# A two-layer hybrid block on one core: weights of products of 256 columns moved 64 bytes off the grid of 256, weight buffers in a strict ring, and VectorE alone updating x behind the output projection

## The chip, the core and the metric

The kernel runs on one core of a Trainium2 chip. The metric is the device time of one execution in microseconds, here the median of three runs. The core's engines work side by side, each through its own list of instructions in order: TensorE (PE in the profile; its weight loads have a line of their own, PEld), VectorE (DVE), ScalarE (ACT), GpSimd (POOL) and SyncE (SP), whose queue issues the weight transfers here.

## The reference

Two layers over 512 tokens of width 1024. Cut to what matters:

```python
h = rms_norm(x, g_pre_mix)
q, k, v, qi, ki, wi, xr, gr, zu, zv, gate_logits = split(h @ w_in)
y_a = dsa_attention(q, k, v, qi, ki, wi)        # indexer picks keys per query
y_b = rg_lru(conv(xr)) * gelu(gr)               # a linear recurrence over tokens
y_c = gelu(zu) * spatial(rms_norm(gelu(zv)))    # masked 128x128 products by chunk
merged = sum_n sigmoid(gate_n) * (y_n @ w_branch_n)
x = x + rms_norm(merged @ w_out, g_post_mix)
f = square(relu(rms_norm(x, g_pre_ffn) @ w_ffn_up)) @ w_ffn_down
x = x + rms_norm(f, g_post_ffn)
x = x + rms_norm((p @ w_ple) * sigmoid(x @ w_ple_gate), g_post_ple)
```

All of it is float32.

## The kernel before

**Layout.** x lies transposed in SBUF: eight tiles X0 to X7 of 128 features by 512 tokens. A product with 128 output columns is a sum over eight k-blocks. To keep float32's precision every operand is split in a high part (rounded to the format that TensorE takes) and the low rest, and each block is three matmuls (`mm3`, L360 to L363): xh·wh, xh·wl, xl·wh. The 128x128 weight block is the operand that is loaded into the array, and the tokens stream through, 512 columns (a wide product) or 256 (a narrow one, half of the tokens). In the spatial products of the gMLP branch it is the other way round: there the weights stream.

**Weights.** A list `order` gives every weight chunk (128x1024, 512 KB) in the order of its use. `prep` (L242) takes the next: a transfer on SP's queue into one of three raw buffers `wr`, a cast on ACT to the high part `wh` (L253) and a subtraction on DVE for the low part `wl` (L254). There are four buffers of each kind (NWB = 4), handed out as they come free, so `wh` and `wl` of one chunk need not lie side by side; chunks of the branches, which serve two products, keep theirs longer while others rotate. All of these tiles, and those that hold x's parts, start at multiples of 512 bytes. `getw(key, ahead)` hands out the weights of the next product and preps up to `ahead` (3) chunks beyond.

**Order of the work.** The program is written in PE's order, with a clock of its own (`clk`, moved on by `tick`) by which deferred pieces are put between the matmuls: `defer(us, fn)` runs `fn` that much later, `run_later` does it. Extra dependencies that cost no waiting (`weights_first`, `behind_products`) keep the scheduler from moving a weight split or a root ahead or back.

**The stage of the change.** Out 0 to 4 of the output projection are wide. Out 5 to 7 go by halves of the tokens (`gemm_halves`, L384): 3 x 24 narrow matmuls for the first 256 tokens, then as many for the others; each of the second three ends with a `prep`. Behind each, `out_evac` squares the sum for the norm's statistics and copies it to Y with the gain (ACT L455 and L1153). When a half is complete, `Norm.complete` gets its 1/rms (`rstd_tok`), brings it to all partitions by two transposes on PE (`rstd_bc`, L497), and starts the generator `x_tiles` (L537), which for tile d writes

```python
V.tensor_mul(ys[d][:, r], ys[d][:, r], bc)              # L544, DVE
(G if d in on_g else V).tensor_add(X[d][:, r], X[d][:, r], ys[d][:, r])  # L547
A.activation(hi, x, AF.Copy, scale=g[:, d:d + 1])       # L557, ACT: xh
st.square(x, r)                                         # L455, ACT
st.accumulate(r)                                        # L461, POOL: sum of squares
V.scalar_tensor_tensor(lo, x, g[:, d:d + 1], f32v(hi), op0=ALU.mult, op1=ALU.subtract)  # L567: xl
```

with the update of tile d + 1 between the square and the accumulation. With `on_g=(1, 3, 5)` POOL does the adds of these three tiles; the accumulations are all POOL's. `gemm_arriving` (L398) takes the tiles as they come for the first four chunks of the FFN's up projection (matmuls L419, 24 narrow ones per chunk and half): three chunks with every tile, the fourth from the second tile on, and the last three tiles of the second half chunk by chunk. The next norm's statistics (`Stats`, L440; `st2` here) are summed alongside. The same two functions serve the last three gate chunks of a layer and the first three chunks (xr 0 to 2) of layer 1.

**Elsewhere.** The recurrence of the RG-LRU branch (L942) runs on ACT and DVE beside the products of the gates and of attention: per feature tile tanh, exp, square, later four square roots in one block (L957). Sigmoid, exp, tanh and root need tables on ACT; a change of table is an ACT_TABLE_LOAD.

Of the kernel before, what the change touches and what calls it, by code (L numbers as in the profile page):

```python
# [9 lines left out]
F32R = mybir.dt.float32r  # L10
# [40 lines left out]
def hybrid_block_kernel(ctx, tc, xT, pT, pos, vec, bsp, freq, w_in, w_tok, w_lru, w_sp, w_br, w_out, w_up, w_dn, w_ple, w_gate, out, depth=DEPTH, dbg=None):  # L51
# [11 lines left out]
    def nm(p):  # L63
        uid[0] += 1
        return f"{p}_{uid[0]}"
# [168 lines left out]
            order.append((("gate", l, d), w_gate[l, d]))  # L234

    prepared = {}
    LA = NWB - 1
    nprep = [0]
    nget = [0]

    def prep():
        weights_first()  # L242
        i = nprep[0]
        nprep[0] += 1
        key, src = order[i]
        raw = wp.tile([128, 1024], F32, tag="wr", name=nm("wr"), bufs=3)
        nc.sync.dma_start(raw, src)
        if key[0] == "sp":
            r3 = raw.rearrange("p (g t) -> p g t", g=8)
            G.affine_select(out=r3, in_=r3, compare_op=ALU.is_ge, fill=0.0, base=0, pattern=[[0, 8], [1, 128]], channel_multiplier=-1)  # L250
        hi = wp.tile([128, 1024], F32R, tag="wh", name=nm("wh"), bufs=NWB)
        lo = wp.tile([128, 1024], F32R, tag="wl", name=nm("wl"), bufs=NWB)
        A.copy(hi, raw)  # L253
        V.tensor_sub(lo, raw, f32v(hi))  # L254
        prepared[key] = (hi, lo)
        if not strict[0]:
            return
        ins = nc.cur_bb.bb.instructions
        parts[:] = [len(ins)] + [next(i.name for i in reversed(ins) if i.engine == e) for e in ENG]
# [125 lines left out]
    def gemm_halves(keys, xs, evac, done):  # L385


        ws = [getw(key, LA if i == 0 else 0) for i, key in enumerate(keys)]
        for r in HALVES:
            for i, w in enumerate(ws):  # L390
                ps = bank()[:, :S // 2]
                gemm(ps, w, xs, KT, r=r)
                evac(i, r, ps)
                if r is HALVES[1] and nprep[0] < len(order):
                    prep()
            done(r)

    def gemm_arriving(keys, xs, source, ranges, arrived=None, lag=LAG, tail=TAIL):  # L398


        n = len(keys)
        ws = [getw(key, 0) for key in keys[:-1]]
        pss = [bank() for _ in keys]
        last = {}
        for r in ranges:
            gen = source(r)
            for k in range(KT):
                with ordered(last):
                    next(gen)
                    todo = [(o, k) for o in range(len(ws))]  # L410
                    if len(ws) < n and k == lag:
                        ws.append(getw(keys[-1], 0))
                        todo += [(n - 1, q) for q in range(k + 1)]
                    if r is ranges[-1] and k >= KT - tail:
                        todo = [] if k < KT - 1 else [(o, q) for o in range(n) for q in range(KT - tail, KT)]
                    for i, (o, q) in enumerate(todo):
                        h3, l3 = [v.rearrange("p (k c) -> p k c", k=KT) for v in ws[o]]
                        for m in range(3):
                            PE.matmul(pss[o][:, r], (h3, l3, h3)[m][:, q], xs[q][m // 2][:, r], start=q == 0 and m == 0, stop=q == KT - 1 and m == 2)  # L419
                        if r is ranges[-1] and q == KT - 1 and o < n - 1:  # L420
                            prep()
                tick(0.65 * len(todo) * width(r) / S)
            if arrived is not None:
                arrived(r)
        while nprep[0] < nget[0] + LA:
            prep()
        return pss
# [12 lines left out]
    class Stats:  # L440


        def __init__(self, late=()):


            self.late = late
            self.n = {}
            self.q = {}
            self.ps = {}
            self.rt = small(4, "rt", 4)  # L450
# [7 lines left out]
        def accumulate(self, r=FULL):  # L458
            n = self.n[r.start, r.stop]
            if 0 < n < (KT - 1 if r in self.late else KT):  # L460
                G.tensor_add(sacc[:, r], sacc[:, r], self.q[r.start, r.stop])  # L461
            self.n[r.start, r.stop] = n + 1

        def add(self, src, r=FULL):
# [109 lines left out]
    chunks = []  # L574
    for key, src in order[:3]:
        raw = wp.tile([128, 1024], F32, tag="wr", name=nm("wr"), bufs=3)
        hi = wp.tile([128, 1024], F32R, tag="wh", name=nm("wh"), bufs=NWB)
        lo = wp.tile([128, 1024], F32R, tag="wl", name=nm("wl"), bufs=NWB)
        prepared[key] = (hi, lo)
        chunks.append((src, raw, hi, lo))  # L580
    nprep[0] = 3
# [19 lines left out]
    for l in range(depth):  # L601
# [544 lines left out]
        yb = [slot("K0", F32, True), slot("K1", F32, True)]  # L1146
        Y = [yb[d // 4][:, d % 4] for d in range(8)]
        st = Stats()
        st2 = Stats()

        def out_evac(d, r, ps):
            st.add(ps, r)
# [2 lines left out]
        for d in range(5):  # L1155
            ps = bank()
            gemm(ps, getw(("out", l, d)), M, KT)
            out_evac(d, FULL, ps)
        norm = Norm(st, D, lambda r, bc: x_tiles(r, XS, vc[:, V_FFN:V_FFN + 8], st2, Y, bc, on_g=(1, 3, 5)))
        gemm_halves([("out", l, d) for d in (5, 6, 7)], M, lambda i, r, ps: out_evac(5 + i, r, ps), norm.complete)  # L1160


        R = cp.tile([128, S], F32, tag="R", name=nm("R"))
        first = gemm_arriving([("up", l, 0, i) for i in range(4)], XS, norm.source, HALVES, st2.row(D, R))
        ps = bank()
        gemm(ps, getw(("up", l, 0, 4)), XS, KT)
        first.append(ps)
        run_later(force=True)
        H = {}
# [168 lines left out]
```

## Time and profile before

| what | value |
|---|---|
| runs | 1815.8, 1817.12, 1817.33 us; median 1817.12 |
| the profiled execution | 1815.54 us |
| its span in the profile | 1813.8 us (1.74 us lie outside it) |
| granted TensorE clock, mean | 0.997 |
| PE busy | 1789.2 us, 99% |
| DVE, ACT, POOL busy | 1149.9 us (63%), 787.3 us (43%), 340.8 us (19%) |
| chain that ended last | PE 75%, DVE 14%, POOL 4%, ACT 4%, issue 3% |
| DMA | 167.75 MB, 92 GB/s in the mean |

How to read it: the span goes from the first to the last recorded instruction. A busy time is the union of the recorded durations; matmuls are pipelined and overlap, so two of them are compared by their starts. A row of the timeline has the start, the duration, engine, line and operation, out<-in by the program's names without buffer numbers, and in brackets the idle time of the engine before it and what ended it. A row of the windows has for each engine the busy time and the number of instructions in the stretch, then the granted clock (1.00 is full), the share of the DMA engines, and GB/s.

### The profile page before, as it was taken

What the parts mean: (1) busy time and instruction counts of PE and PEld (TensorE: products, weight loads), DVE (VectorE), ACT (ScalarE), POOL (GpSimd) and SP (SyncE); (2) the same over time, 40 slices, a digit from 0 to 9 for tenths busy, and PEclk for the clock granted to TensorE, in tenths of its full rate; (3) what the DMA queues carried; (4) which work ended last, traced back from release to release, by engine and by line L of the source; (5) the groups of instructions that cost most, each with busy time, mean ns of one, the idle gap of its engine ahead of it and who ended that gap; (6) DMA issues with size and microseconds to landing.
All of it is one profiled execution on the core that took longest, in us unless ns stands there. A gap on an engine that the chain in (4) does not pass through costs nothing.

```text
span 1813.8 us, 22748 instructions
## 1 busy us (share of the span) xinstructions
PE 1789.2 (99%) x8748; PEld 1497.5 (83%) x8748; DVE 1149.9 (63%) x1946; ACT 787.3 (43%) x1289; POOL 340.8 (19%) x277
## 2 busy tenths in 40 slices
PE   9999999999999999999999999999999999999997
PEld 7888788888988888888888888788889888888886
DVE  8789987656375254534688899876565743544345
ACT  6547246554443222223546473466534422222233
POOL 0612123200420000002454131332004100000033
PEclk9999999999999999999999999999999999999998
DMA  5312322222222232332222222322222323222321
GB/s 176 105 60 97 105 93 94 70 82 82 93 93 94 95 103 93 96 113 86 91 80 99 69 94 84 114 82 70 82 93 70 105 95 103 93 97 102 105 82 58
DMA packets 49676, 167.75 MB, mean 92 GB/s; under 512 B 6048, under 2 KB 8864, under 8 KB 49568
## 3 DMA queue, kind: packets, MB, share of 16 engines
q1 hardware_dynamic: 47376, 163.64, 27.3%
q10 hardware_dynamic: 2192, 2.67, 0.4%
q8 instruction: 68, 1.11, 0.3%
q14 instruction: 40, 0.33, 0.1%
HBM read 164.19 MB, written 2.10 MB: 92 GB/s over the span
## 4 chain that ended last, share of the span: by engine, by line
PE 75%; DVE 14%; POOL 4%; ACT 4%; issue 3%; DMA 0%; SPq 0%; POOLq 0%; ACTq 0%; DVEq 0%
PE ps L361 22%; PE ps L363 22%; PE ps L362 22%; PE ps L419 4%; DVE wl L254 3%; DVE tmp L794 2%; DVE m L792 2%; PE ps L668 2%; PE ps L1060 1%; POOL tmp L653 1%; ACT wh L253 1%; PE ps L1046 1%; POOL sacc L461 1%; PE ps L759 1%; POOL tmp L654 1%
## 5 line engine op out<-in xcount | busy, mean ns | idle before, releaser
L253 ACT CAST wh<-wr 128x1024 fp32r<-128x1024 f32 x303 | 317.2, 1050 | 476.9 <-PE ps L363 397.1
L254 DVE TENSOR_TENSOR wl<-wr,wh 128x1024 fp32r<-128x1024 f32 x303 | 379.2, 1254 | 199.7 <-ACT wh L253 199.3
L361 PE MATMUL ps<-xh,wh 128*128 128x512 f32 (+1 forms) x1296 | 502.5, 388 | 0.0
L363 PE MATMUL ps<-xl,wh 128*128 128x512 f32 (+1 forms) x1296 | 495.4, 382 | 0.0
L362 PE MATMUL ps<-xh,wl 128*128 128x512 f32 (+1 forms) x1296 | 495.2, 382 | 0.0
L363 PEld LDWEIGHTS ps<-xl,wh 128*128 128x128 f32 x1296 | 243.6, 188 | 47.7
L361 PEld LDWEIGHTS ps<-xh,wh 128*128 128x128 f32 x1296 | 243.8, 188 | 45.7 <-issue 1.9
L362 PEld LDWEIGHTS ps<-xh,wl 128*128 128x128 f32 x1296 | 244.1, 188 | 43.3
L461 POOL TENSOR_TENSOR sacc<-sacc,tmp 128x256 f32<-128x256 f32 (+1 forms) x92 | 98.0, 1065 | 884.6 <-issue 584.5
L363 PE MATMUL ps<-V,wh 128*128 128x512 f32 (+1 forms) x528 | 195.4, 370 | 0.0
L363 PE MATMUL ps<-B,wh 128*128 128x512 f32 x336 | 131.1, 390 | 0.0
L361 PE MATMUL ps<-A,wh 128*128 128x512 f32 x320 | 125.0, 390 | 0.0
L362 PE MATMUL ps<-A,wl 128*128 128x512 f32 x320 | 124.5, 389 | 0.0
L1197 DVE TENSOR_TENSOR M<-M,ps 128x512 f32<-128x512 f32 x48 | 33.0, 688 | 141.3 <-PE ps L363 141.3
L1185 DVE TENSOR_TENSOR tmp<-ps,R 128x512 f32<-128x512 f32 x64 | 43.8, 690 | 112.1 <-PE ps L363 109.5
L363 PEld LDWEIGHTS ps<-V,wh 128*128 128x128 f32 x528 | 99.5, 188 | 16.8
L361 PE MATMUL ps<-K,wh 128*128 128x512 f32 x256 | 99.6, 389 | 0.0
L362 PE MATMUL ps<-K,wl 128*128 128x512 f32 x256 | 99.6, 389 | 0.0
L419 PE MATMUL ps<-xl,wh 128*128 128x256 f32 (+1 forms) x264 | 86.2, 326 | 5.5 <-DVE xl L567 5.1
L419 PE MATMUL ps<-xh,wl 128*128 128x256 f32 (+1 forms) x264 | 84.1, 319 | 0.8 <-DVE wl L254 0.8
L419 PE MATMUL ps<-xh,wh 128*128 128x256 f32 (+1 forms) x264 | 84.5, 320 | 0.1
L363 PEld LDWEIGHTS ps<-B,wh 128*128 128x128 f32 x336 | 63.1, 188 | 13.4
(243 smaller groups left out, 2835.7 us busy)
## 6 DMA issues: line engine op xcount, KB each, us to landing
wr<-in_w_in_dram SPq DMA_DIRECT2D x95, 512.0 KB, 3.3
wr<-in_w_up_dram SPq DMA_DIRECT2D x64, 512.0 KB, 3.2
wr<-in_w_dn_dram SPq DMA_DIRECT2D x64, 512.0 KB, 3.2
wr<-in_w_br_dram SPq DMA_DIRECT2D x24, 512.0 KB, 3.2
wr<-in_w_tok_dram SPq DMA_DIRECT2D x16, 512.0 KB, 3.2
wr<-in_w_out_dram SPq DMA_DIRECT2D x16, 512.0 KB, 3.2
wr<-in_w_gate_dram SPq DMA_DIRECT2D x16, 512.0 KB, 3.2
X<-in_xT_dram SPq DMA_DIRECT2D x8, 256.0 KB, 5.7
```

The costliest lines, as they stand in the source:

```text
L253: A.copy(hi, raw)
L254: V.tensor_sub(lo, raw, f32v(hi))
L361: PE.matmul(ps, wh, xh, start=start, stop=False)
L362: PE.matmul(ps, wl, xh, start=False, stop=False)
L363: PE.matmul(ps, wh, xl, start=False, stop=stop)
L419: PE.matmul(pss[o][:, r], (h3, l3, h3)[m][:, q], xs[q][m // 2][:, r], start=q == 0 and m == 0, stop=q == KT - 1 and m == 2)
L461: G.tensor_add(sacc[:, r], sacc[:, r], self.q[r.start, r.stop])
L668: PE.matmul(ps, x, w, start=k == 0 and i == 0, stop=k == KT - 1 and i == 2)
L792: V.max(m8, (sc if r == 0 else wk)[:, :n])
L794: V.match_replace(wk[:, :n], m8, (sc if r == 0 else wk)[:, :n], -3.0e38)
L1185: V.tensor_mul(t, ps, R)
L1197: V.tensor_add(F[d], F[d], ps)
```

## The change

It does four things.

1. *Homes.* `home(key)` replaces the two kinds of buffers by one ring of four, used strictly in turn, high and low part side by side in one tile of 2064 or 2096 columns. Keys in the set `narrow` (spatial, out 5 to 7, gate 5 to 7, up 0 to 3, and in layer 1 xr 0 to 2) start 64 bytes off a multiple of 256 (before or behind it); all others start at a multiple of 256, which in two of the four buffers is 256 past a multiple of 512.
2. *Guests.* Up 1 to 3, the second to fourth weights of the arrival stage, lie in twelve slots that belong to A0 to A7 and B0 to B3, high and low part in two slots each. These slots start at multiples of 512 bytes. Their split is two casts and two subtractions of 128x512.
3. *Splits early.* At the start of the halves of out, `gemm_halves` defers the preps of those three by 0.3, 2.7 and 5.1 us; before, they stood in the second half, one behind each product. The fifth up chunk is fetched with one chunk less ahead.
4. *DVE alone.* `on_g` is dropped for the update behind the output projection, and `st2` sums on DVE.

The diff, cut to its core:

```diff
+    HOMES = [(("A0", "A1"), ("A2", "A3")), (("A4", "A5"), ("A6", "A7")), (("B0", "B1"), ("B2", "B3"))]
+    guests = {}
+    for l in range(depth):
+        guests.update({("up", l, 0, i + 1): HOMES[i] for i in range(3)})
...
+    narrow = set()
+    for l in range(depth):
+        narrow.add(("sp", l))
+        narrow.update(("out", l, d) for d in (5, 6, 7))
+        narrow.update(("gate", l, d) for d in (5, 6, 7))
+        narrow.update(("up", l, 0, i) for i in range(4))
+        if l:
+            narrow.update(("in", l, f"xr{j}") for j in range(3))
+    ring = [0]
+
+    def home(key):
+        i = ring[0] % NWB
+        ring[0] += 1
+        t = wp.tile([128, 2064 if i % 2 else 2096], F32R, tag=f"wp{i}", name=nm("wp"))
+        c = 16 if (key in narrow) == (i % 2 == 0) else 0
+        return t[:, c:c + 1024], t[:, c + 1024:c + 2048]
...
-        hi = wp.tile([128, 1024], F32R, tag="wh", name=nm("wh"), bufs=NWB)
-        lo = wp.tile([128, 1024], F32R, tag="wl", name=nm("wl"), bufs=NWB)
-        A.copy(hi, raw)
-        V.tensor_sub(lo, raw, f32v(hi))
+        if key in guests:
+            hi, lo = [[slot(n, F32R) for n in part] for part in guests[key]]
+            for h in range(2):
+                split(raw[:, h * 512:(h + 1) * 512], hi[h], lo[h])
+        else:
+            hi, lo = home(key)
+            split(raw, hi, lo)
...
         ws = [getw(key, LA if i == 0 else 0) for i, key in enumerate(keys)]
+        n = sum(order[i][0] in guests for i in range(nprep[0], min(nprep[0] + 3, len(order))))
+        for i in range(n):
+            defer(0.3 + 2.4 * i, prep)
         for r in HALVES:
             for i, w in enumerate(ws):
                 ps = bank()[:, :S // 2]
                 gemm(ps, w, xs, KT, r=r)
                 evac(i, r, ps)
-                if r is HALVES[1] and nprep[0] < len(order):
+                if r is HALVES[1] and i >= n and nprep[0] < len(order):
                     prep()
...
-                G.tensor_add(sacc[:, r], sacc[:, r], self.q[r.start, r.stop])
+                self.eng.tensor_add(sacc[:, r], sacc[:, r], self.q[r.start, r.stop])
...
-        st2 = Stats()
+        st2 = Stats(eng=V)
...
-        norm = Norm(st, D, lambda r, bc: x_tiles(r, XS, vc[:, V_FFN:V_FFN + 8], st2, Y, bc, on_g=(1, 3, 5)))
+        norm = Norm(st, D, lambda r, bc: x_tiles(r, XS, vc[:, V_FFN:V_FFN + 8], st2, Y, bc))
...
-        gemm(ps, getw(("up", l, 0, 4)), XS, KT)
+        gemm(ps, getw(("up", l, 0, 4), LA - 1), XS, KT)
```

The scheduler settles where each instruction comes to stand; in all DVE's list grows from 1794 to 1840 rows, ACT's from 1217 to 1231 (six table loads among them), and POOL's shrinks from 282 to 242. Three places. First DVE at the beginning of the update behind layer 0's output projection (K is Y, ps the broadcast of 1/rms, X_176 to X_178 the tiles of x, wl and wr the weights). Before:

```order
L254 TENSOR_TENSOR wl_4352<-wr_4349,wh_4351 128x1024
L490 TENSOR_SCALAR sm_4467<-ps_4464 128x2
L254 TENSOR_TENSOR wl_4480<-wr_4477,wh_4479 128x1024
L544 TENSOR_TENSOR K_872_4172<-K_872_4172,ps_4499 128x256
L547 TENSOR_TENSOR X_176<-X_176,K_872_4172 128x256
L544 TENSOR_TENSOR K_872_4172<-K_872_4172,ps_4499 128x256
L254 TENSOR_TENSOR wl_4518<-wr_4515,wh_4517 128x1024
L567 SCALAR_TENSOR_TENSOR xl_13_188<-X_176,vec_79,xh_12_187 128x256
L544 TENSOR_TENSOR K_872_4172<-K_872_4172,ps_4499 128x256
L547 TENSOR_TENSOR X_178<-X_178,K_872_4172 128x256
L567 SCALAR_TENSOR_TENSOR xl_15_190<-X_177,vec_79,xh_14_189 128x256
L544 TENSOR_TENSOR K_872_4172<-K_872_4172,ps_4499 128x256
```

and after:

```order
L470 TENSOR_TENSOR B_842_4353<-wr_4349,B_840_4351 128x512
L470 TENSOR_TENSOR B_843_4354<-wr_4349,B_841_4352 128x512
L528 TENSOR_SCALAR sm_4417<-ps_4414 128x2
L582 TENSOR_TENSOR K_798_4098<-K_798_4098,ps_4443 128x256
L585 TENSOR_TENSOR X_176<-X_176,K_798_4098 128x256
L582 TENSOR_TENSOR K_798_4098<-K_798_4098,ps_4443 128x256
L585 TENSOR_TENSOR X_177<-X_177,K_798_4098 128x256
L605 SCALAR_TENSOR_TENSOR xl_13_188<-X_176,vec_79,xh_12_187 128x256
L582 TENSOR_TENSOR K_798_4098<-K_798_4098,ps_4443 128x256
L585 TENSOR_TENSOR X_178<-X_178,K_798_4098 128x256
L499 TENSOR_TENSOR sacc<-sacc,tmp_4510 128x256
L605 SCALAR_TENSOR_TENSOR xl_15_190<-X_177,vec_79,xh_14_189 128x256
```

The splits of the up weights (wl_4352 and those behind it) have moved up, in front of the statistics (sm), and lie in slots A and B; tile 1's add is now DVE's, and the sum of squares (sacc) stands in front of each low part.

Second, ACT in the recurrence of layer 0, where weights are cast (wh before, wp after). Before:

```order
L946 ACTIVATE B_338_1619<-B_310_1514,sp_289_1420 128x512
L253 CAST wh_1651<-wr_1649 128x1024
L947 ACT_TABLE_LOAD
L947 ACTIVATE B_310_1514<-B_310_1514,nsp_290_1422 128x512
L949 ACTIVATE tmp_1622<-B_310_1514 128x512
L253 CAST wh_1657<-wr_1655 128x1024
```

and after:

```order
L983 ACTIVATE B_312_1593<-B_284_1488,sp_266_1397 128x512
L469 CAST wp_1619<-wr_1617 128x1024
L984 ACT_TABLE_LOAD
L984 ACTIVATE B_284_1488<-B_284_1488,nsp_267_1399 128x512
L986 ACTIVATE tmp_1596<-B_284_1488 128x512
L469 CAST wp_1694<-wr_1692 128x1024
L469 CAST wp_1629<-wr_1627 128x1024
```

Between the weights 1619 and 1629 (1651 and 1657 before) a cast for a product further on, 1694 (1723 before, ten rows further down), has come to stand.

Third, ACT some rows further on, with the square roots of the recurrence (L957 before, L994 after) and a gate's tanh (L919, L956). Before:

```order
L253 CAST wh_1723<-wr_1721 128x1024
L949 ACTIVATE tmp_1707<-B_332_1603 128x512
L957 ACT_TABLE_LOAD
L957 ACTIVATE B_338_1619<-B_338_1619 128x512
L957 ACTIVATE B_353_1664<-B_353_1664 128x512
L957 ACTIVATE B_355_1682<-B_355_1682 128x512
L957 ACTIVATE B_359_1704<-B_359_1704 128x512
L919 ACT_TABLE_LOAD
L919 ACTIVATE tmp_1770<-tmp_1770 128x512
```

and after:

```order
L994 ACTIVATE B_312_1593<-B_312_1593 128x512
L956 ACT_TABLE_LOAD
L956 ACTIVATE tmp_1668<-tmp_1668 128x512
L984 ACTIVATE B_306_1577<-B_306_1577,nsp_267_1399 128x512
L994 ACT_TABLE_LOAD
L994 ACTIVATE B_324_1635<-B_324_1635 128x512
L986 ACTIVATE tmp_1678<-B_306_1577 128x512
L994 ACTIVATE B_326_1653<-B_326_1653 128x512
L956 ACT_TABLE_LOAD
L956 ACTIVATE tmp_1740<-tmp_1740 128x512
L994 ACT_TABLE_LOAD
L994 ACTIVATE B_330_1675<-B_330_1675 128x512
```

The four roots stood behind one table load; now they stand apart, with loads between them for tanh and exp.

## Rows read from the trace of the kernel before

**Rows 1.** The page, busy time of the engines (share of the span, instructions).

```profile
PE 1789.2 (99%) x8748; PEld 1497.5 (83%) x8748; DVE 1149.9 (63%) x1946; ACT 787.3 (43%) x1289; POOL 340.8 (19%) x277
```

**Rows 2.** Windows of stages; columns: window, length, busy (count) of PE, PEld, DVE, ACT, POOL, PEclk, DMA.

```profile
471.00:489.00 18.00, 18.00 (x152) 17.99 (x151) 4.75 (x7) 8.82 (x18) 6.38 (x8) 1.00 0.22 79
489.00:515.00 26.00, 24.59 (x199) 23.88 (x198) 23.00 (x44) 15.95 (x36) 18.09 (x21) 1.00 0.12 41
900.00:925.00 25.00, 21.49 (x153) 18.84 (x152) 22.42 (x44) 14.41 (x37) 19.38 (x23) 1.00 0.18 58
160.00:180.00 20.00, 20.00 (x90) 16.57 (x89) 18.13 (x37) 18.60 (x26) 5.89 (x5) 1.00 0.29 102
200.00:225.00 25.00, 23.56 (x102) 18.54 (x101) 23.96 (x39) 6.65 (x10) 4.98 (x4) 1.00 0.32 106
```

**Rows 3.** Timeline of PE, wide products; columns: start, duration (us), engine, line, operation.

```profile
470.32 0.39 PE L361 MATMUL ps<-M,wh 128*128 128x512 f32 x1
...
471.00 0.28 PE L361 MATMUL ps<-M,wh 128*128 128x256 f32 x1
```

**Rows 4.** Timeline of PE, narrow products of the output projection.

```profile
478.08 0.28 PE L363 MATMUL ps<-V,wh 128*128 128x256 f32 x1
...
478.80 0.28 PE L363 MATMUL ps<-V,wh 128*128 128x256 f32 x1
```

**Rows 5.** Timeline of PE, weight loads with two columns streamed each, near the end.

```profile
1794.31 0.59 PE L471 MATMUL ps<-ones,tmp 128*128 128x2 f32 x4
1794.76 0.36 PE L361 MATMUL ps<-xh,wh 128*128 128x256 f32 x1
```

**Rows 6.** Timeline of PE, the broadcast in the halves of out, and the matmul behind them.

```profile
484.76 0.38 PE L497 MATMUL ps<-ident,rt 128*128 128x128 f32 x2
...
488.92 0.28 PE L419 MATMUL ps<-xh,wh 128*128 128x256 f32 x1
```

**Rows 7.** Timeline of DVE, update of x behind the output projection, layer 0.

```profile
486.02 0.42 DVE L544 TENSOR_TENSOR K<-K,ps 128x256 f32<-128x256 f32 x1
486.47 0.42 DVE L547 TENSOR_TENSOR X<-X,K 128x256 f32<-128x256 f32 x1
486.81 0.41 DVE L544 TENSOR_TENSOR K<-K,ps 128x256 f32<-128x256 f32 x1
...
489.21 0.47 DVE L567 SCALAR_TENSOR_TENSOR xl<-X,vec,xh 128x256 fp32r<-128x256 f32 x1
489.61 0.41 DVE L544 TENSOR_TENSOR K<-K,ps 128x256 f32<-128x256 f32 x1
...
490.58 0.47 DVE L567 SCALAR_TENSOR_TENSOR xl<-X,vec,xh 128x256 fp32r<-128x256 f32 x1
...
510.20 1.35 DVE L567 SCALAR_TENSOR_TENSOR xl<-X,vec,xh 128x256 fp32r<-128x256 f32 x2
```

**Rows 8.** Timeline of ACT, same stage: a cast of weights, the square of X1.

```profile
489.76 1.05 ACT L253 CAST wh<-wr 128x1024 fp32r<-128x1024 f32 x1
490.70 0.42 ACT L455 ACTIVATE tmp<-X 128x256 f32<-128x256 f32 x1
```

**Rows 9.** Timeline of DVE, the last update of x.

```profile
1805.68 1.27 DVE L546 SCALAR_TENSOR_TENSOR B<-B,gp,ps 128x256 f32<-128x256 f32 x3 [1.35 <-PE ps L497]
```

**Rows 10.** Timeline of ACT, recurrence of layer 0: a table load.

```profile
173.32 1.28 ACT L957 ACT_TABLE_LOAD   x1
```

**Rows 11.** Timeline of DVE, same stretch: low parts of two of those weights.

```profile
167.44 1.21 DVE L254 TENSOR_TENSOR wl<-wr,wh 128x1024 fp32r<-128x1024 f32 x1
...
180.35 1.22 DVE L254 TENSOR_TENSOR wl<-wr,wh 128x1024 fp32r<-128x1024 f32 x1
```

**Rows 12.** Timeline of PE, same stretch: first reads of those low parts.

```profile
170.61 0.39 PE L362 MATMUL ps<-xh,wl 128*128 128x512 f32 x1
...
184.21 0.39 PE L362 MATMUL ps<-V,wl 128*128 128x512 f32 x1
```

More of the change, by code (lines that the diff above doesn't have):

```diff
@@ L236, in hybrid_block_kernel, with part @@
     prepared = {}
+    HOMES = [(("A0", "A1"), ("A2", "A3")), (("A4", "A5"), ("A6", "A7")), (("B0", "B1"), ("B2", "B3"))]
+    guests = {}
+    for l in range(depth):
+        guests.update({("up", l, 0, i + 1): HOMES[i] for i in range(3)})
+    def part(w, k):
+        if isinstance(w, list):
+            return w[k // 4][:, (k % 4) * 128:(k % 4 + 1) * 128]
+        return w[:, k * 128:(k + 1) * 128]
     LA = NWB - 1
@@ L416, in gemm_arriving @@
                     for i, (o, q) in enumerate(todo):
-                        h3, l3 = [v.rearrange("p (k c) -> p k c", k=KT) for v in ws[o]]
+                        hi, lo = [part(v, q) for v in ws[o]]
                         for m in range(3):
-                            PE.matmul(pss[o][:, r], (h3, l3, h3)[m][:, q], xs[q][m // 2][:, r], start=q == 0 and m == 0, stop=q == KT - 1 and m == 2)
+                            PE.matmul(pss[o][:, r], (hi, lo, hi)[m], xs[q][m // 2][:, r], start=q == 0 and m == 0, stop=q == KT - 1 and m == 2)
                         if r is ranges[-1] and q == KT - 1 and o < n - 1:
@@ L440, in hybrid_block_kernel, with __init__ @@
     class Stats:
-        def __init__(self, late=()):
+        def __init__(self, late=(), eng=G):
+            self.eng = eng
             self.late = late
@@ L576, in hybrid_block_kernel @@
         raw = wp.tile([128, 1024], F32, tag="wr", name=nm("wr"), bufs=3)
-        hi = wp.tile([128, 1024], F32R, tag="wh", name=nm("wh"), bufs=NWB)
-        lo = wp.tile([128, 1024], F32R, tag="wl", name=nm("wl"), bufs=NWB)
+        hi, lo = home(key)
         prepared[key] = (hi, lo)
```

## The prediction

> **What bounds the kernel now.** The page comes first: TensorE is busy for 99% of the span [rows 1], so time is saved only by shorter matmuls or by the few waits left. Next come the windows of the stages in which x arrives tile by tile [rows 2]: behind the output projection of layer 0 (489 to 515) PE is busy 24.59 of 26 us and VectorE (DVE) 23.00, in the arrival of layer 1's first products (900 to 925) PE 21.49 of 25 and DVE 22.42. Both stages are tight on two engines. Last comes the timeline of PE, read from start to start, because the busy times of pipelined matmuls overlap. A product of 512 columns takes three matmuls in 471.00 - 470.32 = 0.68 us, 226.7 ns each [rows 3]. One of 256 columns takes six in 478.80 - 478.08 = 0.72 us, 120 ns each [rows 4]. Half of the wide price would be 113.3 ns, so the narrow ones pay 6.7 ns more per column block. What paces them? Near the end four weight loads go through with only two columns streamed behind each: 1794.76 - 1794.31 = 0.45 us, 112.5 ns each [rows 5]. A load that stands almost alone thus costs 112.5 ns, and 120 when 256 columns stream beside it. I read this as a narrow product being bound by its weight load, with 7.5 ns of disturbance by the stream.
>
> **Part one: narrow weights 64 bytes off.** The same instructions run; only the spacing can change. The bounds: nothing below (0 ns), and above 13.3 ns, since the two prices give 226.7 - 120 = 106.7 ns for 256 further columns and no matmul is likely to undercut its own stream. I take 7.5 ns, the load that runs alone [rows 5], as the row nearest to a load that nothing disturbs. There are 912 such matmuls: 144 in the halves of out and 144 in those of gate per layer, 48 of up 0 and 48 of the spatial products per layer, 144 of layer 1's xr. Where each stands decides what it is worth.
>
> - *Halves of gate, layer 1, to the end.* The last update of x waits for PE [rows 9], so all 144 count: 144 x 7.5 = 1.1 us.
> - *Halves of gate, layer 0, to layer 1's arrivals.* The update is DVE's there [rows 2] and begins behind the broadcast in the halves. In out's halves, which the same code writes, that stands at 484.76 [rows 6], (484.76 - 471.00) / 0.12 = 115 matmuls behind their start [rows 3]: 115 x 7.5 = 0.9 us. What xr saves itself is lost again behind DVE.
> - *Halves of out.* In layer 0 they end at 488.92 [rows 6], and would end 1.1 us earlier; the worth comes with part two.
> - *Spatial products:* nothing. They lie before the attention and indexer stage, where DVE is busy 23.96 of 25 us [rows 2], and its pace takes 0.4 us back.
>
> A rule speaks against part one. By the Trainium skill, "TensorE: Matmul & The Clock Gate", Part 2, step 1 on LDWEIGHTS, the array has two independent read ports, so that loading the next weights takes no read bandwidth from the running matmul; by it an address would not matter, and the 120 ns would stay. The rows do not settle it, since no load of the kernel before stands off its grid beside a narrow stream.
>
> **Part two: the update of x behind the output projection.** It removes the three adds and the seven accumulations per half from POOL, adds them to DVE, and takes three weight splits out of the stage (casts on ACT, low parts on DVE, both earlier, where DVE has the room: from 471 to 489 it is busy 4.75 of 18 us [rows 2]). [Rows 7] give DVE's pitch: multiply to dependent add 486.47 - 486.02 = 0.45, add to the next 0.34, low part to the next 489.61 - 489.21 = 0.40. An accumulation has the add's shape, 0.34. A tile then costs 0.45 + 0.34 + 0.34 + 0.40 = 1.53 us on DVE. PE has 12 matmuls a tile, 12 x 0.12 = 1.44. So DVE, not PE, paces the stage.
>
> Where does the chain start? The low part of tile 1 comes at 490.58 [rows 7]. It will stand behind accumulation 1, which needs ACT's square of X1, at 490.70 now because ACT first evacuates out 7 and then casts a weight at 489.76 [rows 8]. Without the cast the square follows the evacuation, 489.76; with halves 1.1 us shorter, 488.65; plus 0.42 for the square, 0.34 for the accumulation and some 0.1 of hand-over, low part 1 comes at 489.5, 1.1 us earlier. From there: low part 1, 0.40; five whole tiles, 7.65; tile 7 without its next update, 0.74; that is 498.3. The second half: first update 0.79, tile 0 without accumulation 1.19, six tiles 9.18, the last 0.74; 510.2. Now the last two low parts end at 511.55 [rows 7]. Gain 1.35 us; the 32 matmuls behind them stay. I take 1.3 us per layer, the two layers running the same code. With no effect of the offset the chain starts 1.1 later, and part two alone is worth 0.2 per layer.
>
> POOL's contribution falls away at no cost, because nothing else waits for it there. The cast and low parts of the guests move to the start of the halves, their DMA issues on SP with them, about 2.4 us apart by the deferral; they take the slots A and B, idle at that time, and each raw buffer is free again once split. I cost this at nothing: the idle 13 us of DVE from 471 to 489 hide it. Were the cover gone, one low part, 1.22 us [rows 11], would fall on the path.
>
> **Part three, unasked: buffers in a strict ring.** High and low part share a buffer, and buffers come in order. ACT then casts weight 1694, for a later product, ahead of 1629, and the roots of the recurrence no longer stand in one block: from row to row the table changes, six loads more in all (four in layer 0, two in layer 1). One costs 1.28 us [rows 10], on an ACT busy for 18.60 of 20 us there [rows 2]. Two prices. The weight behind 1694 comes a cast and a low part later, 1.05 + 1.21 = 2.26 us, while its low part, ended at 168.65 [rows 11], has 1.96 us until PE reads it at 170.61 [rows 12]: a stall of 0.3, up to 0.9 if the buffer itself comes late. Three more tables stand before the next cast, 3.84 us; that weight's low part ends at 181.57 [rows 11] and is read at 184.21 [rows 12], slack 2.64: up to 1.2 us. Both stalls of layer 0 lie ahead of a stage where PE already waits for DVE, busy 23.56 of 25 us [rows 2], so 1.44 us of it can be absorbed. I take 0, with -1 and +2 as ends.
>
> **Sum.** 2 x 1.3 + 0.9 + 1.1 = 4.6 us. The profiled execution took 1815.54 us (span 1813.8 and 1.74 around it), so 1810.9 by its measure; it lies 1.58 us under the median of 1817.12, so I forecast 1812.5 for the median. 0.2% of it is 3.6 us, about what a measurement of this kernel can tell: the bounds are 1813.5 and 1820.8.
>
> **The rivals.**
>
> 1. *The offset does nothing.* For it: 120 ns in every narrow group whatever the address, and the rule above. Against it: the 112.5 ns of a load alone. Part two is left, 2 x 0.2, and the ring's -1 to +2: 1815.7 to 1818.7, about 1816.7.
> 2. *PE paces the update.* If DVE's accumulations hide better than by their pitch, the stage is 192 matmuls of 0.12 from the halves' end at 487.8: 23.0 and 0.7 for the first tiles, end at 511.5, where the window of the stage is cut at 515 [rows 2]. That is 3.5 per layer, 2.2 more than I took: 1808.1, and with 10 ns for the offset on the 576 matmuls of the halves, 1.4 less, 1806.7. Against it: 1.53 against 1.44 us a tile.
> 3. *Slower: ACT's tables hold the weights.* If the stage behind does not absorb them, 0.9 + 1.2 us in layer 0 fall on PE, and the same in layer 1: 4.2 us, less the 0.4 of part two where the offset gives nothing, 1820.9. It decides when a weight's low part ends after PE's need of it by more than 1 us in both layers. For it: ACT's 18.60 of 20 us. Against it: DVE, not ACT, sets the later stage.
> 4. *Wide products suffer.* In two of four buffers they now start at 256 past a multiple of 512, which no wide product does before. One nanosecond on 3000 of the 8748 matmuls [rows 1] is 3 us, so two of them would bury the gain: 1818.5, and three 1821.5. Nothing in the rows points to it.
> 5. *The change doesn't do what it says*, in part: ups 1 to 3 sit in slots on the old grid, and only up 0 gains there. It is in the sum already.
>
> **Chances.** Forecast 0.46 (1810.5 to 1815, by part three's ends and 5 to 10 ns; three quarters of it under 1813.5), rival 1 0.22, rival 2 0.16, rival 3 0.11, rival 4 0.05. Faster: 0.35 + 0.16 = 0.51; same: 0.11 + 0.22 = 0.33; slower: rivals 3 and 4, 0.16. The range reaches from rival 2 with its larger gain, 1806.5, to 1819.5; above it lie rival 4 and most of rival 3.
>
> **What would show it.** Narrow matmuls of out, six in under 0.69 us in place of 0.72, and wide ones still three in 0.68: part one. DVE in 489 to 512 nearly without idle time, the low parts some 1.53 us apart, and PE waiting a little at every tile: part two. No PE wait for a low part of weights near 170 and 184: part three. Six in 0.72 would make the forecast wrong by 4 us, and a wide pitch above 227 ns in half the buffers by more.

## The result and the profile after

The change made the kernel slower: 1838.11 us in the median (1835.41 to 1840.7, 4 runs) against 1817.22 (1815.8 to 1817.59, 4 runs). The measured ratio is 1.0118, 95% interval [1.0105, 1.0131]; the two medians alone give 1.0115. I had forecast 1812.5. The profiled execution took 1835.41 us with a span of 1833.7; its mean granted clock is 0.993, 0.997 before.

The page of the changed kernel, its line of busy times (engine, us, share, instructions) and the chain that ended last, by engine; the first answers to [rows 1]:

```profile
PE 1796.2 (98%) x8748; PEld 1501.1 (82%) x8748; DVE 1160.4 (63%) x1992; ACT 798.2 (44%) x1301; POOL 305.9 (17%) x237
...
PE 82%; DVE 12%; issue 2%; ACT 2%; POOL 2%; DMA 0%; SPq 0%; ACTq 0%; POOLq 0%; DVEq 0%
```

PE is busy 7.0 us longer with the same 8748 matmuls and its share falls from 99 to 98%: part of the loss is standing still, part is slower work. Both programs hold the same matmuls, and all but some 130 of the 8748 start in the same order, so I compared the starts of the matmuls place by place in the two traces. What each stretch adds to the delay:

| stretch (times of before) | us |
|---|---|
| start to 66 | +0.2 |
| 66 to 187: gMLP, recurrence of layer 0 | +5.7 |
| 187 to 319: what follows gives back | -2.1 |
| 319 to 380: attention, layer 0 | +8.4 |
| 470 to 488: halves of out, layer 0 | -0.5 |
| 488 to 514: arrival of x at up, layer 0 | +0.4 |
| 514 to 927: FFN, halves of gate, arrivals of layer 1 | -0.3 |
| 927 to 1224 | +0.6 |
| 1224 to 1286: attention, layer 1 | +8.4 |
| 1286 to 1412: up to the halves of out and the arrival at up, layer 1 | -0.1 |
| 1782 to the end: halves of gate, last update | -0.7 |

The sum is 20.0; the span is 19.9 longer. The 17 us in attention and the 5.7 before it lie far from what the change is about. The windows of the changed kernel (window, length, busy and count of PE, PEld, DVE, ACT, POOL, granted clock, DMA share, GB/s) show two things at each place; 500 to 526 answers to the window 489 to 515 of [rows 2]:

```profile
160.00:170.00 10.00, 6.75 (x24) 4.84 (x23) 9.83 (x21) 8.41 (x12) 1.79 (x2) 0.86 0.33 105
325.00:335.00 10.00, 10.00 (x51) 7.97 (x50) 3.00 (x4) 1.25 (x2) 1.28 (x1) 1.00 0.11 36
335.00:345.00 10.00, 7.58 (x31) 5.93 (x31) 5.92 (x19) 6.44 (x19) 0.37 (x1) 0.83 0.33 105
365.00:375.00 10.00, 8.58 (x44) 6.68 (x42) 2.74 (x4) 2.44 (x4) 1.29 (x1) 1.00 0.26 94
375.00:385.00 10.00, 9.01 (x36) 7.21 (x37) 6.56 (x21) 5.92 (x19) 1.28 (x1) 0.83 0.17 54
500.00:526.00 26.00, 23.95 (x196) 23.23 (x196) 22.70 (x59) 15.16 (x34) 2.37 (x3) 1.00 0.00 1
1240.00:1250.00 10.00, 7.58 (x30) 5.71 (x28) 5.59 (x17) 5.63 (x15) 0.00 (x0) 0.83 0.32 107
```

From 335 to 345 PE is busy for 7.58 us only, and the clock granted is 0.83 in the mean: part of the time it was at the lower of its two levels (1.2 and 2.4 GHz), and 0.17 of 10 us, 1.7 us of work at full speed, is lost. The clock falls alike at 375 and at 1240 (0.83) and at 160 (0.86). Weight chunks have names here: g1_6 is chunk 6 of gate 1, br1.2 chunk 2 of branch 1, lru the recurrence's. ACT's timeline shows what PE stood for:

```profile
332.47 1.05 ACT L469 CAST wp<-wr 128x1024 fp32r<-128x1024 f32 x1 [7.27 <-PE ps L397]
335.19 1.04 ACT L469 CAST wp<-wr 128x1024 fp32r<-128x1024 f32 x1 [1.66 <-PE ps L397]
336.14 0.47 ACT L469 CAST tmp<-ps 128x384 fp32r<-128x384 f32 x1
```

And PE's, of the same stretch:

```profile
334.76 0.39 PE L397 MATMUL ps<-B,wp 128*128 128x512 f32 x1
336.66 0.45 PE L1097 MATMUL ps<-tmp,V 128*128 128x256 f32 x2 [1.51 <-ACT tmp L469]
338.01 0.69 PE L1097 MATMUL ps<-tmp,V 128*128 128x256 f32 x2 [0.90 <-DVE tmp L470]
...
339.03 0.63 PE L396 MATMUL ps<-xh,wp 128*128 128x512 f32 x1
339.46 0.63 PE L397 MATMUL ps<-xl,wp 128*128 128x512 f32 x1
339.89 0.63 PE L395 MATMUL ps<-xh,wp 128*128 128x512 f32 x1
```

ACT is not busy there, it stands. The second cast of weights (chunk g1_6) waits until 335.19, because in the ring its buffer is the one of the branch chunk br1.2, whose last read on PE starts at 334.76. PE first needs g1_6 at 354.16, nineteen microseconds later. But behind that cast, in order, stands the small cast of probabilities at 336.14, and that one PE needs now: it stands 1.51 us, takes the high parts, and stands 0.90 us more for DVE's low part. Then its matmuls of 512 columns come 0.43 us apart (339.03, 339.46, 339.89), in place of 0.227 [rows 3]. In the kernel before the second cast of weights stood behind the small one:

```profile
328.74 1.05 ACT L253 CAST wh<-wr 128x1024 fp32r<-128x1024 f32 x1 [7.27 <-PE ps L363]
329.69 0.47 ACT L432 CAST tmp<-ps 128x384 fp32r<-128x384 f32 x1
331.90 1.05 ACT L253 CAST wh<-wr 128x1024 fp32r<-128x1024 f32 x1 [1.74 <-PE ps L363]
```

The first of these is g1_6, in the buffer that came free first; br1.3 waits, behind the small cast.

In the recurrence it is a weight itself that comes late. ACT's casts:

```profile
150.95 1.06 ACT L469 CAST wp<-wr 128x1024 fp32r<-128x1024 f32 x1
157.38 0.63 ACT L956 ACTIVATE tmp<-tmp 128x512 f32<-128x512 f32 x1 [5.37 <-DVE tmp L955]
...
162.48 1.03 ACT L469 CAST wp<-wr 128x1024 fp32r<-128x1024 f32 x1
```

And PE:

```profile
163.56 0.50 PE L395 MATMUL ps<-xh,wp 128*128 128x512 f32 x1 [0.76 <-ACT wp L469]
166.56 0.50 PE L396 MATMUL ps<-xh,wp 128*128 128x512 f32 x1 [2.49 <-DVE wp L470]
...
167.86 0.63 PE L397 MATMUL ps<-xl,wp 128*128 128x512 f32 x1
168.29 0.63 PE L395 MATMUL ps<-xh,wp 128*128 128x512 f32 x1
```

At 150.95 ACT casts br2.1, which PE first reads at 173.50. Chunk g2_2, which PE needs before 163, follows at 162.48: in the ring it has the buffer of the recurrence's weights (lru), whose last read starts at 151.53, and br2.1 has the one whose last read started at 148.81. So br2.1 got the early place in ACT's list, and g2_2 the next one, which lies behind work that waits for DVE, 5.37 us at 157.38 alone. PE stands 0.76 and 2.49 us, and then works at the lower clock, 0.43 us apart. The kernel before gave g2_2 the buffer that was free first: its cast at 150.38 is g2_2's and the one at 161.91 br2.1's.

### The profile page after: what moved, and what is told of

Same layout as the page of the kernel before. It is cut to its first block, busy times and chain, and to the rows that moved or that the text cites. A ratio compares the mean times of both kernels' runs of the same rounds, so it can differ in the third digit from the quotient of the medians.

```text
span 1833.7 us, 22716 instructions
## 1 busy us (share of the span) xinstructions
PE 1796.2 (98%) x8748; PEld 1501.1 (82%) x8748; DVE 1160.4 (63%) x1992; ACT 798.2 (44%) x1301; POOL 305.9 (17%) x237
## 4 chain that ended last, share of the span: by engine, by line
PE 82%; DVE 12%; issue 2%; ACT 2%; POOL 2%; DMA 0%; SPq 0%; ACTq 0%; POOLq 0%; DVEq 0%
PE ps L395 23%; PE ps L397 23%; PE ps L396 23%; PE ps L456 5%; PE ps L705 3%; DVE wp L470 2%; DVE tmp L831 2%; DVE m L829 2%; PE ps L1097 1%; PE ps L1083 1%; DVE tmp L908 1%; PE ps L796 1%; ACT wp L469 1%; PE ps L782 1%; DVE tmp L812 1%
## 5 line engine op out<-in xcount | busy, mean ns | idle before, releaser
L469 ACT CAST wp<-wr 128x1024 fp32r<-128x1024 f32 (+2 forms) x306 | 314.7, 1033 | 508.6 <-PE ps L397 425.0
L470 DVE TENSOR_TENSOR wp<-wr,wp 128x1024 fp32r<-128x1024 f32 (+2 forms) x306 | 373.4, 1224 | 210.9 <-ACT wp L469 210.3
L395 PE MATMUL ps<-xh,wp 128*128 128x512 f32 (+1 forms) x1296 | 504.5, 389 | 0.8 <-ACT wp L469 0.8
L396 PE MATMUL ps<-xh,wp 128*128 128x512 f32 (+1 forms) x1296 | 497.6, 384 | 2.5 <-DVE wp L470 2.5
L397 PE MATMUL ps<-xl,wp 128*128 128x512 f32 (+1 forms) x1296 | 497.4, 384 | 0.0
L397 PEld LDWEIGHTS ps<-xl,wp 128*128 128x128 f32 x1296 | 245.0, 189 | 48.7 <-issue 0.4
L395 PEld LDWEIGHTS ps<-xh,wp 128*128 128x128 f32 x1296 | 245.2, 189 | 47.1 <-issue 1.7
L396 PEld LDWEIGHTS ps<-xh,wp 128*128 128x128 f32 x1296 | 245.1, 189 | 46.9 <-DVE wp L470 3.2
L397 PE MATMUL ps<-V,wp 128*128 128x512 f32 (+1 forms) x528 | 195.0, 369 | 0.0
L397 PE MATMUL ps<-B,wp 128*128 128x512 f32 x336 | 130.9, 390 | 0.0
L395 PE MATMUL ps<-A,wp 128*128 128x512 f32 x320 | 125.0, 391 | 0.0
L396 PE MATMUL ps<-A,wp 128*128 128x512 f32 x320 | 124.5, 389 | 0.0
L395 PE MATMUL ps<-K,wp 128*128 128x512 f32 x256 | 99.6, 389 | 0.0
L396 PE MATMUL ps<-K,wp 128*128 128x512 f32 x256 | 99.6, 389 | 0.0
L456 PE MATMUL ps<-xh,wp 128*128 128x512 f32 (+1 forms) x336 | 85.7, 341 | 0.1
```

The source lines that it names most:

```text
L395: PE.matmul(ps, wh, xh, start=start, stop=False)
L396: PE.matmul(ps, wl, xh, start=False, stop=False)
L397: PE.matmul(ps, wh, xl, start=False, stop=stop)
L456: PE.matmul(pss[o][:, r], (hi, lo, hi)[m], xs[q][m // 2][:, r], start=q == 0 and m == 0, stop=q == KT - 1 and m == 2)
L469: A.copy(hi, src)
L470: V.tensor_sub(lo, src, f32v(hi))
```

## The experiments

Each was timed beside the kernel before on the same chip; the ratios are against it. Several chips were used, so experiments are better compared by their ratios than by their times.

**1. The ring alone.** The kernel before with this and no more:

```diff
-        hi = wp.tile([128, 1024], F32R, tag="wh", name=nm("wh"), bufs=NWB)
-        lo = wp.tile([128, 1024], F32R, tag="wl", name=nm("wl"), bufs=NWB)
+        i = ring[0] % NWB
+        ring[0] += 1
+        t = wp.tile([128, 2048], F32R, tag=f"wp{i}", name=nm("wp"))
+        hi, lo = t[:, 0:1024], t[:, 1024:2048]
```

> The kernel before with nothing but the strict ring: four buffers, high and low part side by side, handed out in turn, every start on the old grid of 512 bytes, no offset, no guests, POOL as before. Theory ring (in the ring ACT's casts of weights come to stand ahead of small casts that TensorE needs, TensorE stands, and its granted clock falls): about 1838 us, +20, with the waits of the changed kernel near 165, 337, 375, 1245 and 1283 us and a granted clock of 0.83 in windows of 10 us there. Rival early splits (the guests and DVE's longer list displace ACT's work): 1817, no such waits. Rival addresses: 1817.

Measured: 1838.95 us, 1.0122 [1.0108, 1.0135]. The whole loss is there, without an offset, a guest or a moved instruction of the update. Attention costs 9.9 us in layer 0 and 11.2 in layer 1, by the starts of the matmuls.

**2. The update alone.** The change with `home` giving separate buffers on the old grid, as they come free:

```diff
-        t = wp.tile([128, 2064 if i % 2 else 2096], F32R, tag=f"wp{i}", name=nm("wp"))
...
+        return [wp.tile([128, 1024], F32R, tag=t, name=nm(t), bufs=NWB) for t in ("wh", "wl")]
```

> The change without its first part: guests, early splits and DVE alone in the update behind the output projection, but buffers as before, handed out as they come free, and no start off the grid. Theory ring: no long waits in the recurrence or in attention; the out/up stage alone differs, by 1 us per layer to the worse, since the changed kernel lost about 1 us there net of the 0.75 that the narrow matmuls saved: about 1819. Rival early splits: about 1837 to 1840. My prediction before the result would have had 1816.7.

Measured: 1817.29 us, 1.0005 [0.9996, 1.0014]. No long waits, so early splits displace nothing. By the matmuls' starts the stage from the halves of out to the end of the arrival is 0.6 us longer than before in each layer; the whole is no difference that can be measured. My expectation of 1819 was too high, and the prediction's price for part two alone, 0.2 better per layer, has the wrong sign in the trace.

**3. The offset alone.** The kernel before, buffers joint and off the grid as in the change, but taken in the order in which the kernel before took its own:

```diff
+    PLAN = ("01230123...")
...
+        i = seat[key]
+        t = wp.tile([128, 2064 if i % 2 else 2096], F32R, tag=f"wp{i}", name=nm("wp"))
+        c = 16 if (key in narrow) == (i % 2 == 0) else 0
```

> The kernel before with the 64 bytes off for narrow weights, all four up chunks included, and joint buffers taken in the order in which the kernel before took its buffers (a list of buffer numbers in place of the ring); POOL keeps its share and the splits stay late. Theory ring: no long waits; six narrow matmuls in 0.68 to 0.70 us in place of 0.72, 0.75 us off each of the four groups of halves, of which the arrivals of layer 1 give back 0.2: 1814.0 to 1815.5. Rival addresses (the offset or the wide starts at 256 past a multiple of 512 cost): above 1817.

Measured: 1814.67 us, 0.9991 [0.9982, 1.0]: faster, at the edge of what can be told. No stall of the ring is left, though high and low parts share a buffer here too: it is the strict turn that costs, not the sharing. One new wait came in, which delays the matmuls by 1.2 us, for a low part in the products after the indexer of layer 0:

```profile
236.98 0.50 PE L383 MATMUL ps<-xh,wp 128*128 128x512 f32 x1 [0.97 <-DVE wp L275]
```

**4. The whole change with the old order of buffers.** As the diff of 3, in the changed kernel.

> The whole change, except that the ring is replaced by the order of buffers of the kernel before (a list of buffer numbers). Theory ring: all 20 us come back, and what is left is the offset's gain of some 2.5 us less the loss of about 1 us per layer in the out/up stage: 1816 to 1818, granted clock 0.997. Rival early splits: still 1835 or more.

Measured: 1816.0 us, 1.0 [0.9991, 1.0009], clock 0.997. All of the loss is back and the rest of the change is worth nothing that can be measured; the offset's gain is spent on the update and on the wait of 3.

**5. Two exchanges in the ring.** Experiment 1 with two pairs of chunks of layer 0's attention in each other's buffers, g1_6 with br1.3 and (n = 61 and 62) g0_2 with g0_3, not g0_1 with g0_2 as the expectation has it:

```diff
+        if n in (56, 61):
+            p, q = n % NWB, (n + 1) % NWB
+            seats[p], seats[q] = seats[q], seats[p]
+        i = seats[n % NWB]
```

> The ring alone, with two exchanges of neighbours in layer 0's attention: the chunks g1_6 and br1.3, and g0_1 and g0_2 behind them, take each other's buffers (and the ring goes on with the labels exchanged). Theory ring, in its narrow form (a cast of weights that waits for a buffer still being read stands on ACT ahead of the small cast of probabilities that TensorE needs next): layer 0's attention loses its two stalls with their fall of the clock, some 8 to 10 us; layer 1's stalls stay as control: 1829 to 1831. Rival (the ring's delay comes from anywhere else in its order, or from joint buffers): 1837 to 1840.

Measured: 1828.86 us, 1.0071 [1.0057, 1.0085], against 1.0122 for the ring alone 9 to 10 us less. ACT's list shows what the exchange did at the first place, ring alone on the left (614 is br1.3, 593 g1_6):

```
ring alone                        with the exchange
CAST wp_614  128x1024             CAST wp_593  128x1024
CAST wp_593  128x1024             CAST tmp_595 128x384
CAST tmp_595 128x384              CAST wp_614  128x1024
```

And on the chip, ACT at that place:

```profile
333.46 1.05 ACT L265 CAST wp<-wr 128x1024 fp32r<-128x1024 f32 x1 [7.26 <-PE ps L375]
334.41 0.47 ACT L444 CAST tmp<-ps 128x384 fp32r<-128x384 f32 x1
336.63 1.05 ACT L265 CAST wp<-wr 128x1024 fp32r<-128x1024 f32 x1 [1.75 <-PE ps L375]
```

The small cast comes at 334.41, right behind the first cast of weights, and the second one waits where it harms nobody. Windows of the two places in layer 0, and of one in layer 1, where nothing was exchanged:

```profile
335.00:345.00 10.00, 10.00 (x53) 8.15 (x53) 8.03 (x23) 7.66 (x21) 1.30 (x1) 1.00 0.34 107
375.00:385.00 10.00, 10.00 (x50) 8.29 (x49) 4.95 (x10) 5.07 (x12) 0.00 (x0) 1.00 0.31 105
1275.00:1285.00 10.00, 9.16 (x31) 7.25 (x32) 5.70 (x21) 5.42 (x17) 1.28 (x1) 0.66 0.15 52
```

PE's waits in the attention of layer 1 of the same run (what waited, for what, us in total, times, longest):

```profile
PE ps L1071 <- ACT tmp L444: 3.0, 2, 1.5
PE ps L1071 <- DVE tmp L445: 1.8, 2, 0.9
```

In layer 0 PE is busy all the time at full clock, and no wait is listed; in layer 1 the four waits and the clock of 0.66 are still there. The matmuls of layer 0's attention, 9.9 us late in the ring alone, lose 0.0 here. This shows the mechanism at its place.

**6. 32 bytes off.** Experiment 3 with `c = 8` for narrow weights.

> As offset_alone, but narrow weights 32 bytes off a multiple of 256 in place of 64. If it is enough that the load starts off the grid of the stream, six narrow matmuls late in a group take 0.68 us as with 64 bytes; if 64 bytes are needed, 0.72. The rest of the trace as offset_alone.

Measured, in one run: a pitch between the two expected. In the first half of out 7:

```profile
479.80 0.28 PE L382 MATMUL ps<-M,wp 128*128 128x256 f32 x1
...
481.10 0.28 PE L384 MATMUL ps<-V,wp 128*128 128x256 f32 x1
```

Eleven steps in 1.30 us, 118 ns. With 64 bytes the changed kernel has, in the same half of out 7:

```profile
490.63 0.28 PE L396 MATMUL ps<-M,wp 128*128 128x256 f32 x1
...
491.77 0.28 PE L397 MATMUL ps<-V,wp 128*128 128x256 f32 x1
```

Ten steps in 1.14 us, 114 ns, where it was 120 [rows 4]. How far the address is off matters, and here 64 bytes are better than 32.

**7. Early splits with POOL at work.** Experiment 4 with `on_g=(1, 3, 5)` and `st2 = Stats()` put back.

> seats_of_before with the update of x shared with POOL as in the kernel before (its three adds and the sums of squares): offset and early splits, without DVE alone. If the late splits cost the stage (wl at 487.96 and 491.31 lie on the chain of waits before), it ends 1 to 2 us earlier per layer than in offset_alone: 1812 to 1813.5. Rival: POOL's adds of 0.74 to 0.93 us pace the stage then: 1814.5 to 1816.

Measured: 1819.41 us, 1.0016 [1.0007, 1.0025]: slower, a miss, and the most useful run. From the start of out's halves to the end of the arrival 2.2 us were gained in layer 0 (and 2.1 in layer 1), and then PE stood at the transposes of the norm's 1/rms, in layer 0 and in layer 1:

```profile
519.44 0.43 PE L544 MATMUL ps<-ident,rt 128*128 128x128 f32 x2 [2.29 <-POOL rt L538]
...
1418.49 0.43 PE L544 MATMUL ps<-ident,rt 128*128 128x128 f32 x2 [2.18 <-POOL rt L538]
```

ACT and DVE before the first of them:

```profile
516.22 1.05 ACT L478 CAST wp<-wr 128x1024 fp32r<-128x1024 f32 x1 [2.84 <-DMA wr<-in_w_up_dram]
517.30 1.23 DVE L479 TENSOR_TENSOR wp<-wr,wp 128x1024 fp32r<-128x1024 f32 x1 [2.30 <-ACT wp L478]
518.44 0.15 DVE L537 TENSOR_SCALAR sm<-ps 128x2 f32<-128x2 f32 x1
```

The statistics on DVE (L537) take 0.15 us, but stand in order behind a weight's low part (up 7's) that waited 2.30 us for ACT's cast, and that cast had waited 2.84 us for its weight's transfer. In the kernel before, the scheduler put the same low part behind the statistics:

```profile
516.52 0.15 DVE L490 TENSOR_SCALAR sm<-ps 128x2 f32<-128x2 f32 x1
...
519.33 1.23 DVE L254 TENSOR_TENSOR wl<-wr,wh 128x1024 fp32r<-128x1024 f32 x1 [0.16 <-ACT wh L253]
```

In layer 1, other than in layer 0, the clock fell after the wait (0.83 from 1415 to 1425), and the loss is 3.9 us.

**8. The same, the transposes later.** One number:

```diff
-        first = gemm_arriving([("up", l, 0, i) for i in range(4)], XS, norm.source, HALVES, st2.row(D, R))
+        first = gemm_arriving([("up", l, 0, i) for i in range(4)], XS, norm.source, HALVES, st2.row(D, R, pick=6.0))
```

> early_splits_pool with one number more: the two transposes that bring the FFN norm's 1/rms to all partitions stand 6.0 us of program time behind its statistics in place of 1.7. Reading: in early_splits_pool the stage of the up products ends 2.2 us earlier per layer and then TensorE waits 2.3 us (3.9 in layer 1) at these transposes, since DVE computes the statistics only behind a weight's low part whose cast comes late. With the transposes later both gains stay: 6 us under early_splits_pool, 1812 to 1814. Rival (the products behind need that row at once, so the wait only changes its place): 1817 to 1819.

Measured: 1812.3 us, 0.9978 [0.9969, 0.9987]. The transposes pass without a wait, now all four together:

```profile
520.78 0.60 PE L544 MATMUL ps<-ident,rt 128*128 128x128 f32 x4
```

This version beats both kernels: 0.22% under the one before, and by the ratios some 25 us under the change.

**9. The same with the sums of squares on DVE.**

> As early_late_row, with the sums of squares on DVE and the three adds on POOL. DVE then has 0.45 + 0.34 + 0.40 + 5/8 of 0.34 = 1.40 us a tile, just under TensorE's 1.44: if pitch alone decides, the same time as early_late_row within 1 us. Rival (DVE stretched by POOL's adds, as rows of 0.5 to 0.6 us beside POOL show, and standing in order behind ACT's squares): 1 to 3 us more per layer.

Measured: 1815.43 us, 0.9995 [0.9986, 1.0004]: 3.1 us above experiment 8, 1.6 per layer. The rival holds, pitch alone does not decide; which of the rival's two reasons does, this run doesn't tell.

**10. DVE alone with late splits.** Experiment 3 with the change's `Stats(eng=V)` and without `on_g`.

> offset_alone with DVE alone in the update behind the output projection, the splits staying late: DVE's 1.52 us a tile and three low parts of 1.22 us besides: 2 to 3 us per layer above seats_of_before: 1819 to 1822. If DVE has more room there than I read, 1816.

Measured: 1819.67 us, 1.0021 [1.0012, 1.003], as expected. By the matmuls' starts the arrival stage loses 1.8 us in layer 0 and 3.2 in layer 1. The ratios price both: DVE alone costs 0.30%, 5.4 us (1.0021 against 0.9991 in experiment 3), and the early splits with their guests give back 0.21%, 3.8 us of it (1.0 in experiment 4).

## Why the prediction was wrong

**The step that failed is part three.** "I take 0, with -1 and +2 as ends" for the strict ring; it cost 1.22%, some 22 us (experiment 1). I read one exchange of casts and three more table loads in the recurrence off the order, and sized them by the next weights' own waits, 0.3 to 0.9 and up to 1.2 us. Three things were missing. First, the pair that mattered stood six rows above the first that I showed: the cast there belonged to g2_2 in the kernel before, and had become one for br2.1. Cast 1619, which I set against 1651, is g2_2's, and 1651 is br2.1's. I compared positions of casts and not which weight each was for, and when its buffer came free. Second, I never asked for the stages where branch chunks hold their buffer for two products, which are the very places where a ring in turn and a choice of the free buffer differ: attention was in no term. Third, I priced a late weight only by its own reader, not by what stands behind it on ACT: g1_6 had 19 us to spare, the small cast behind it none. And I had no term for the clock: its fall adds 1.7 us to the 1.51 and 0.90 us that PE stands at each such place, 4.1 us, and there are two such places in each attention.

**Rival 3 was on the right side for a wrong reason.** It blamed the six table loads (in the profile ACT has 12 instructions more, 1289 to 1301: these six and six casts of the guests' halves) and put the stalls near 170 and 184. The ring alone has the same 23 loads as the change, but so has experiment 5, where the loss in layer 0's attention is gone; the stalls came at 163 and 166, from a weight that was cast too late, and at four places in attention, which the rival does not have. Its price of 4.2 us was a fifth.

**Part one held in kind, not in size.** Narrow matmuls come at 113 ns (forecast 112.5), but in the halves of out and gate only from the 25th to 50th on; before that they come at 118, and in out's halves of layer 0 another two dozen do so behind the statistics' small products and the transposes. So 144 of them saved 0.5 us in out and 0.75 in the last gate halves, not 1.1. In layer 0's gate halves 0.5 us were saved, and 0.2 of it was lost again behind DVE in layer 1's arrivals, as the prediction had it in kind. Rival 1 falls: the pitch goes with the address of the weights. In the arrival stage of the changed kernel both prices stand side by side, with the same tile of x as the moving operand, first up 0's weights (wp, 64 bytes off), then up 1's (A, on the grid of 512):

```profile
506.26 0.39 PE L456 MATMUL ps<-xh,wp 128*128 128x256 f32 x2
...
506.60 0.40 PE L456 MATMUL ps<-xh,A 128*128 128x256 f32 x2
...
506.96 0.28 PE L456 MATMUL ps<-xh,A 128*128 128x256 f32 x1
```

Three matmuls of up 0 take 0.34 us, 113 ns each, and three of up 1 0.36, 120 each. By the rule of the Trainium skill ("TensorE: Matmul & The Clock Gate", Part 2, step 1, LDWEIGHTS) that loading the next weights takes no read bandwidth from the running matmul, the address would not matter, as the prediction reads it. It does for these float32 products, 120 against 113 ns, and the measurement decides; whether the load or the stream gives way, no run separates. Rival 4 falls too: wide matmuls whose weights start 256 past a multiple of 512 come at 227 ns like the others, over some 3200 of them.

**Part two: the pitch was right, the sum was not.** DVE in the update of the changed kernel:

```profile
503.72 0.48 DVE L605 SCALAR_TENSOR_TENSOR xl<-X,vec,xh 128x256 fp32r<-128x256 f32 x1
...
504.93 0.16 DVE L528 TENSOR_SCALAR sm<-ps 128x2 f32<-128x2 f32 x1 [0.40 <-PE ps L509]
...
505.67 0.48 DVE L605 SCALAR_TENSOR_TENSOR xl<-X,vec,xh 128x256 fp32r<-128x256 f32 x1
...
507.20 0.48 DVE L605 SCALAR_TENSOR_TENSOR xl<-X,vec,xh 128x256 fp32r<-128x256 f32 x1
...
515.77 0.16 DVE L528 TENSOR_SCALAR sm<-ps 128x2 f32<-128x2 f32 x1 [0.25 <-PE ps L509]
...
522.59 0.48 DVE L605 SCALAR_TENSOR_TENSOR xl<-X,vec,xh 128x256 fp32r<-128x256 f32 x1
...
523.57 0.48 DVE L605 SCALAR_TENSOR_TENSOR xl<-X,vec,xh 128x256 fp32r<-128x256 f32 x1
```

Low parts come at 503.72, 505.67 and 507.20, the last two 1.53 us apart, as forecast, and DVE is busy for 22.70 of the 26 us (23.00 before, [rows 2]). I missed that the statistics of the other half stand on DVE between the tiles and wait for PE (504.93 and 515.77, idle 0.40 and 0.25 besides), which makes the first of these steps 1.95 us, and that the last accumulation waits for ACT's last square, so that the last two low parts are 0.98 us apart, where I had 0.74. Together with a low part of tile 1 that came 0.5 us later than my 489.5 (502.20, less the 12.2 us that the kernel was late by then), the chain ended about 1.6 us behind my sum, and a gain of 0.2 per layer without the offset became a loss of 0.6 (experiment 2). Rival 2, PE as the pace, is not reached with DVE alone. What was worth something is the half that I took for a detail: with early splits and POOL still adding (experiments 7 and 8) the stage ends 2.2 us earlier in layer 0, 0.7 of which the offset alone gives (experiment 3). The prediction's 0.1 us of hand-over stands in no row; it is too small to matter here.

**Absorption** was right in kind: of the 5.7 us that layer 0 lost up to the recurrence, 2.1 came back in the stage that DVE bounds, where I had put 1.44. But in attention nothing behind it gave anything back.

Two things stay open: why the joint buffers in the old order bring a wait of 1.2 us at 237 (experiments 3 and 4) that separate ones don't have, and what the table loads cost by themselves. No run tells.

## What to carry to other kernels

When a change touches who gets which buffer, list for each chunk three times: when its buffer's last reader ends, when its load or cast stands in line, and when it is first needed. A ring in strict turn is only as good as its longest tenant; and what a waiting cast costs is not its own lateness but that of everything behind it on an in-order engine. When a stage is made shorter, look at the next small thing in line (here a 0.15 us statistic) and at what the scheduler has put in front of it (a weight's low part, whose transfer came late).

## What the runs showed of the hardware

- The pitch of narrow float32 matmuls depends on the address of the loaded weights: 120 ns on the grid of 512, 118 with 32 bytes off a multiple of 256 (one run), and with 64 bytes two levels, in the halves of out and gate 118 at the beginning and 113 after 24 to 48 matmuls. For wide ones, 227 ns, the start at 256 past 512 makes no difference.
- PE's granted clock fell to the lower level after it stood 1.51 and 0.90 us with two matmuls between them (336.66, 338.01), and 0.76 and 2.49 with one between (163.56, 166.56). After one wait of 2.29 us (519.44, experiment 7) the clock stayed at 1.00 from 515 to 525, but after one of 2.18 us at the same place of layer 1 (1418.49, same run) it fell, to a mean of 0.83 from 1415 to 1425: the length of a wait alone doesn't tell. In the arrival stage of the changed kernel, 500 to 526, it stayed at 1.00 with three waits, 2.0 us in all.
